# One layout for RWKV's block operands, its state part as 64-row products, and constant products ahead of others, in a hybrid encoder layer

## Chip, cores and metric

The kernel runs on one core of one Trainium2 chip. The metric is device microseconds (us) of one execution. Five engines work side by side, each in its own order: TensorE (PE in the profile; PEld is its weight loading), VectorE (DVE), ScalarE (ACT), GpSimd (POOL) and SyncE (SP), which issues most DMAs. TensorE's clock is granted at one of two levels, 1.2 or 2.4 GHz; "PEclk" in the profile is the mean granted clock of a stretch as a share of 2.4 GHz.

## What is computed

One encoder layer on 2048 tokens of width 1024, all in float32. Four mixers of 256 columns run on the projected input, their outputs are projected and added to x, and a mixture of 16 experts (each expert takes 256 tokens) follows.

```python
proj = jnp.einsum('btd,dc->btc', _rmsnorm(x, norm_mix[l]), w_in[l])
o_ret  = _retention_group(...)     # chunked retention, both directions
o_rwkv = _rwkv7_group(...)         # RWKV-7, both directions
o_lru  = _rglru_group(...)         # linear recurrence
o_gla  = _gla_group(...)           # gated linear attention, both directions
x = x + concat([o_ret, o_rwkv, o_lru, o_gla]) @ w_out[l]
x = x + _expert_choice_ffn(_rmsnorm(x, norm_ffn[l]), ...)
return _rmsnorm(x, norm_final)

# RWKV, one direction, per token and head (64 x 64 state S):
sa = jnp.einsum('bhvk,bhk->bhv', S, -kk_t)
S  = S * w_t[:, :, None, :] + sa[..., None] * (kk_t * a_t)[:, :, None, :] + v_t[..., None] * k_t[:, :, None, :]
y  = jnp.einsum('bhvk,bhk->bhv', S, r_t)
```

## The kernel before

The program is a series of stages: input projection, the linear recurrence, RWKV's first part (woven with more projection), then the stage that the change touches, then the output projection, the choice of tokens (`top_k`) and the experts.

The stage that the change touches weaves three generators with fixed weights: `rwkv_rest` (RWKV's second part, then the split of w_out and the first four tiles of the output projection), `retention` and `gla`. Each `yield` is a point at which the weave may go on with another generator. A scheduler then orders each engine's instructions from this list by its own estimate of readiness, so the order within an engine is fixed when the program is built; each engine executes its list in order and waits on semaphores.

RWKV's second part works on 16 blocks of 128 tokens (two chunks of 64) in two directions, so on 32 pairs (direction, block). `rwkv_load` fetches a pair's operands. `rwkv_prep` builds its matrix E in steps: p1 (four transposes, line 606), p2 (four transposes, line 615), R (four products on 64 rows of the array, line 628), the inner masks (four whole-array products, line 639), X (line 648) and E (four products of 256 columns, line 656). After each step ACT or DVE copies from the PSUM bank into the operand of a later step; before the change most of these copies work on 64 of the 128 partitions at a time, since the two chunks' halves lie crosswise (lines 610, 618, 633, 643). E = q1 - X q0, where q1 holds, beside computed parts, a constant identity and a DMA'd copy of r. `rwkv_chain` carries the state: per chunk four products E times mv (line 672), then a DVE product into the next mv (line 676) and an ACT copy of the output (line 680). RWKV has four PSUM banks of its own in rotation, retention and GLA two each.

A float32 product is executed in two passes and appears in the trace as two matmul records and two weight loads; a transpose as one.

Of the kernel before, what the change touches and what calls it, by code (L numbers as in the profile page):

```python
# [17 lines left out]
P = 128  # L18
# [4 lines left out]
NH = 4  # L23
# [513 lines left out]
def rwkv_b_buffers(g):  # L537

    nc = g.nc

    engines = [nc.vector, nc.gpsimd]

    def ring(name, shape, n, parts):
        ts = [g.fp.tile(shape, F32, name=f"{name}{i}") for i in range(n)]
        for i, t in enumerate(ts):
            for p in parts(t):
                engines[0].memset(p, 0.0)
                engines.reverse()
        return [ts, 0]

    def eye(t):
        for k, t1 in ((0, t[0:64, :, 0, 64:128]), (1, t[64:128, :, 1, 0:64])):
            nc.scalar.activation(out=t1, in_=g.c["eye64"][64 * k:64 * k + 64, None, :].broadcast_to([64, NH, C]), func=AF.Copy)
        return []
    g.rd = ring("rd", [P, 4, 2, C], 2, lambda t: [t[64 * k:64 * k + 64, :, 1 - k, :] for k in range(2)])
    g.q0 = ring("q0", [P, NH, 2, P], 2, lambda t: [t[64 * e:64 * e + 64, :, 1 - e, :] for e in range(2)])
    g.q1 = ring("q1", [P, NH, 2, P], 4, eye)
    g.ti = ring("ti", [P, NH, P], 4, lambda t: [t[64 * e:64 * e + 64, :, 64 - 64 * e:128 - 64 * e] for e in range(2)])
    g.mv = {}
# [7 lines left out]
def rwkv_load(g, dr, b):  # L567
# [14 lines left out]
    return ld, q1, ti  # L582


def rwkv_prep(g, dr, b, loaded, res):

    nc, c = g.nc, g.c
    ld, q1, ti = loaded  # L590
# [12 lines left out]
    for q in range(2):
        for e in range(2):
            o = (2 * q + e) * P
            nc.tensor.transpose(p1[:, o:o + P], bk[q][e], c["ident"])
    p1 = p1.rearrange("p (q e h c) -> p q e h c", q=2, e=2, h=2)
    for e in range(2):
# [3 lines left out]
    p2 = bank(g)  # L612
# [8 lines left out]
    rd = turn(g.rd)  # L621
    for k in range(2):
        nc.vector.tensor_copy(out=rd[H[k], :, k], in_=ld[H[k]].rearrange("p (u t) -> p u t", t=320)[:, :, 0:C])
    pss = [bank(g) for _ in range(2)]
    for q in range(2):
        for k in range(2):
            ks = ld[H[k], HALF * q:HALF * q + 384].rearrange("p (u t) -> p u t", t=C)[:, 1::3]
            nc.tensor.matmul(pss[k][:, q * P:(q + 1) * P], lhsT=z[q][H[k]], rhs=ks, start=True, stop=True)  # L628
    for k in range(2):
        pv = pss[k][:, 0:256].rearrange("p (q e t) -> p q e t", q=2, e=2)  # L630
        for e in range(2):
            s = H[e]
            nc.vector.tensor_tensor(out=R[s, k::2, H[1 - e]], in0=pv[s, :, 1 - e], in1=c["m_bm"][s, dr, None, :].broadcast_to([64, 2, C]), op=OP.mult)
    yield
    ps = bank(g)
    for q in range(2):
        for e in range(2):
            o = (2 * q + e) * P
            nc.tensor.matmul(ps[:, o:o + P], lhsT=bk[q][e], rhs=rd[:, 2 * q + 1 - e], start=True, stop=True)  # L639
    pv = ps.rearrange("p (q e h t) -> p q e h t", q=2, e=2, h=2)  # L640
    for e in range(2):
        for s, q in ((H[e], q0), (H[1 - e], q1)):
            nc.vector.tensor_tensor(out=qh(q[s, :, e, H[e]]), in0=pv[s, :, e], in1=c["m_in"][s, dr, None, None, :].broadcast_to([64, 2, 2, C]), op=OP.mult)
    yield

    ps = bank(g)
# [5 lines left out]
    E = g.ep.tile([P, NH, 2, P], F32, name="E", tag="E")  # L652
    for h2 in range(2):
        ps = bank(g)
        for h in range(2):
            nc.tensor.matmul(ps[:, h * 256:(h + 1) * 256], lhsT=X[:, 2 * h2 + h, :], rhs=q0[:, 2 * h2 + h].rearrange("p e c -> p (e c)"),  # L656
                             start=True, stop=True)
        s = slice(2 * h2, 2 * h2 + 2)
        nc.vector.tensor_tensor(out=E[:, s].rearrange("p h e c -> p (h e c)"), in0=q1[:, s].rearrange("p h e c -> p (h e c)"), in1=ps, op=OP.subtract)
        yield  # L660
# [1165 lines left out]
```

## Time and profile before

| | us |
|---|---|
| median of three runs | 2861.12 (2857.55 to 2868.86) |
| the profiled execution | 2858.58 |
| its span, first to last instruction | 2856.6 |
| RWKV's second part (lines 571 to 683) | from 836 to 1291 of the span |
| first and last matmul of the output projection | 1352.8 and 1626 |
| `top_k` begins, then the experts | 1633 |

Over the span PE is busy 91%, DVE 61%, ACT 49%, POOL 25%, and the mean granted clock is 0.947. Before 836 PE is busy 754 of 836 us and after 1633 it is busy 1162 of 1224 us, at 0.96 and 0.97 of the full clock. Between them the share of busy time and the clock are both lower. The section of rows below gives this stretch in six pieces. A busy share is to be read with the clock beside it, since a matmul at the lower clock is busy for longer. A piece of the PE timeline is a run of records of one line; the distance from its start to the start of the next piece, divided by its records, is what a record costs in the stream.

### The profile page before, as it was taken

To read this page: it belongs to the slowest core of one execution; us is meant where nothing else is said; L and a number is where in the kernel's file an instruction comes from. 1 tells how busy PE (TensorE), PEld (TensorE's weight loads), DVE (VectorE), ACT (ScalarE), POOL (GpSimd) and SP (SyncE) were. 2 spreads that over 40 slices of the span, in tenths; PEclk is the share of its full clock that TensorE was granted. 3 is DMA by queue.
4 is the path that set the end of the run, shared out by engine and by line. 5 is a ranking of instruction groups with operands and counts; after the bars stand their busy time and mean duration, and the time that the engine had idled before them with its cause. 6 is when DMAs were issued, how large, how long until landed. Compare 5 with 4: busy or idle time off the path is not lost.

```text
span 2856.6 us, 47428 instructions
## 1 busy us (share of the span) xinstructions
PE 2594.7 (91%) x18433; PEld 2321.6 (81%) x18433; DVE 1746.1 (61%) x3415; ACT 1392.3 (49%) x2348; POOL 711.5 (25%) x771
## 2 busy tenths in 40 slices
PE   6989998989888888886979859999999999999997
PEld 5866787768767777774767659999999999999987
DVE  4454567766887667788443475555555555566564
ACT  4366555435434676555533334444444444455453
POOL 0011115443524454347433200000000000000121
PEclk9999999999988889997989979999999999999999
DMA  8735554675446544446344346666666666789873
GB/s 304 278 101 190 182 164 151 203 231 166 136 122 177 161 153 148 145 127 190 107 143 171 127 147 206 205 206 205 206 205 205 205 206 206 228 289 298 266 238 140
DMA packets 474015, 538.40 MB, mean 188 GB/s; under 512 B 129952, under 2 KB 411584, under 8 KB 473024
## 3 DMA queue, kind: packets, MB, share of 16 engines
q1 hardware_dynamic: 461984, 492.12, 53.3%
q0 software_dynamic: 11808, 43.26, 5.8%
q8 instruction: 145, 2.38, 0.3%
q14 instruction: 78, 0.64, 0.1%
HBM read 392.17 MB, written 145.23 MB: 188 GB/s over the span
## 4 chain that ended last, share of the span: by engine, by line
PE 53%; DVE 5%; DMA 4%; ACT 3%; issue 2%; POOL 1%; SPq 0%; POOLq 0%; ACTq 0%; DVEq 0%
PE bank L129 43%; DMA rt_ld<-tm 1%; PE bank L656 1%; PE bank L1500 1%; PE bank L639 1%; DMA fn_x<-acc,x_idx 1%; PE bank L628 1%; PE bank L672 1%; PE bank L1481 1%; PE bank L648 1%; DVE tk_j L1395 0%; PE bank L1217 0%; PE bank L1323 0%; PE bank L960 0%; PE bank L952 0%
## 5 line engine op out<-in xcount | busy, mean ns | idle before, releaser
L44 DVE TENSOR_TENSOR x_wl<-x_st,x_wh 128x2048 fp32r<-128x2048 f32 x192 | 439.5, 2292 | 306.3 <-ACT x_wh L43 305.9
L129 PE MATMUL bank<-x_xh,x_wh 128*128 128x256 f32 x2048 | 580.2, 285 | 2.9 <-ACT x_wh L43 2.8
L129 PE MATMUL bank<-x_xl,x_wh 128*128 128x256 f32 x2048 | 577.4, 283 | 0.0
L129 PE MATMUL bank<-x_xh,x_wl 128*128 128x256 f32 x2048 | 572.2, 283 | 1.1 <-DVE x_wl L44 1.1
L43 ACT ACTIVATE x_wh<-x_st 128x2048 fp32r<-128x2048 f32 x192 | 367.0, 1913 | 106.7 <-PE bank L129 96.6
L129 PEld LDWEIGHTS bank<-x_xh,x_wh 128*128 128x128 f32 x2048 | 393.2, 192 | 3.6 <-ACT x_wh L43 3.2
L129 PEld LDWEIGHTS bank<-x_xl,x_wh 128*128 128x128 f32 x2048 | 393.3, 192 | 0.0
L129 PEld LDWEIGHTS bank<-x_xh,x_wl 128*128 128x128 f32 x2048 | 389.9, 192 | 1.5 <-DVE x_wl L44 1.5
L129 PE MATMUL bank<-x_wh,x_hh 128*128 128x256 f32 x1024 | 290.1, 285 | 4.8 <-ACT x_hh L43 4.8
L129 PE MATMUL bank<-x_wl,x_hh 128*128 128x256 f32 x1024 | 291.2, 285 | 0.0
L129 PE MATMUL bank<-x_wh,x_hl 128*128 128x256 f32 x1024 | 289.8, 284 | 0.0
L1626 POOL DMA_INDIRECT acc<-x_os,x_idx x30 | 48.9, 1631 | 926.8 <-ACT x_os L1560 899.0
L129 PE MATMUL bank<-h_hi,w_hi 128*128 128x512 f32 x576 | 238.5, 417 | 20.1 <-DVE o_cm L1676 13.8
L129 PE MATMUL bank<-h_lo,w_hi 128*128 128x512 f32 x576 | 240.0, 417 | 0.0
L129 PE MATMUL bank<-h_hi,w_lo 128*128 128x512 f32 x576 | 235.6, 409 | 0.0
L129 PEld LDWEIGHTS bank<-x_wh,x_hh 128*128 128x128 f32 x1024 | 196.6, 193 | 5.0 <-ACT x_hh L43 5.0
L129 PEld LDWEIGHTS bank<-x_wl,x_hh 128*128 128x128 f32 x1024 | 197.4, 193 | 0.0
L129 PEld LDWEIGHTS bank<-x_wh,x_hl 128*128 128x128 f32 x1024 | 197.2, 193 | 0.0
L129 PE MATMUL bank<-w_hi,h_hi 128*128 128x256 f32 (+1 forms) x512 | 156.4, 306 | 14.6 <-DVE o_tm L1676 11.8
L129 PEld LDWEIGHTS bank<-h_hi,w_hi 128*128 128x128 f32 x576 | 112.5, 196 | 56.3 <-DVE o_cm L1676 16.4
L129 PE MATMUL bank<-w_lo,h_hi 128*128 128x256 f32 (+1 forms) x512 | 149.4, 292 | 0.0
L129 PE MATMUL bank<-w_hi,h_lo 128*128 128x256 f32 (+1 forms) x512 | 148.8, 291 | 0.0
(457 smaller groups left out, 5490.2 us busy)
## 6 DMA issues: line engine op xcount, KB each, us to landing
x_st<-in_exp_w_gate_dram SPq DMA_DIRECT2D x64, 1024.0 KB, 8.4
x_st<-in_exp_w_up_dram SPq DMA_DIRECT2D x64, 1024.0 KB, 8.9
x_st<-in_exp_w_down_dram SPq DMA_DIRECT2D x64, 1024.0 KB, 5.5
w_st<-in_w_in_dram SPq DMA_DIRECT2D x20, 1024.0 KB, 6.7
rw_sp<-sp SPq DMA_DIRECT2D x16, 1280.0 KB, 4.6
bld<-rw_sp SPq DMA_DIRECT2D x32, 640.0 KB, 4.1
ld<-rw_cm SPq DMA_DIRECT2D x14, 899.5 KB, 6.1
cm<-o_cm SPq DMA_DIRECT2D x40, 256.0 KB, 2.8
```

The lines of the kernel that those rows point to most:

```text
L43: g.nc.scalar.activation(out=hi, in_=src, func=AF.Copy)
L44: (g.nc.gpsimd if pool else g.nc.vector).tensor_tensor(out=lo, in0=src, in1=hi.bitcast(F32), op=OP.subtract)
L129: g.nc.tensor.matmul(out, lhsT=lhs[a][:, k, lsl], rhs=rhs[b][:, k, rsl], start=(k + i == 0 and out is outs[0]), stop=(3 * k + i == 3 * nk ...
L628: nc.tensor.matmul(pss[k][:, q * P:(q + 1) * P], lhsT=z[q][H[k]], rhs=ks, start=True, stop=True)
L639: nc.tensor.matmul(ps[:, o:o + P], lhsT=bk[q][e], rhs=rd[:, 2 * q + 1 - e], start=True, stop=True)
L648: nc.tensor.matmul(ps[:, h * P:(h + 1) * P], lhsT=ti[:, h], rhs=R[:, h], start=True, stop=True)
L656: nc.tensor.matmul(ps[:, h * 256:(h + 1) * 256], lhsT=X[:, 2 * h2 + h, :], rhs=q0[:, 2 * h2 + h].rearrange("p e c -> p (e c)"), start=True ...
L672: nc.tensor.matmul(ps[:, h, :], lhsT=E[:, h, e, :], rhs=mv[e][:, h, :], start=True, stop=True)
L1481: nc.tensor.matmul(ps[:, 2 * s:2 * s + 2], lhsT=oh[:, i, s * P:(s + 1) * P], rhs=tok[:, i], start=(i == 0), stop=(i == NB - 1))
L1500: nc.tensor.transpose(ps[:, m * CAP + s * P:m * CAP + (s + 1) * P], xs[:, s, (k + m) * P:(k + m + 1) * P], c["ident"])
L1626: g.nc.gpsimd.indirect_dma_start(out=dst, out_offset=bass.IndirectOffsetOnAxis(ap=idx[:, s:s + 1], axis=0), in_=t[:, s], in_offset=None, **kw)
```

## The change

A helper `full` issues one bfloat16 product of 128 x 512 on a view of the identity into a bank, before the real products overwrite that bank. It stands ahead of six of the eight banks of `rwkv_prep` and of three per block of `retention` and of `gla`: 192 + 48 + 48 = 288 products.

In `rwkv_prep` the operands lie the same way on all 128 partitions: Q replaces q0 and q1, one copy replaces four (p1), one replaces two (R's left part), two products replace four (R's right part), one replaces four (masks). Per pair ACT issues 5 copies in place of 9, DVE 5 in place of 12. The two DVE copies into `rd` become two DMAs (64 in all) in `rwkv_load`. The R products become eight of 64 x 64, the E products sixteen of 64 x 64 with 128 columns. The constant identity and r leave E: `rwkv_chain` adds their part as products, per chunk one of `eye64` with 256 columns, four of `rq` with 64, and eight of E (128 rows, 64 columns of the array) where four whole-array products stood.

```diff
+def full(g, ps):
+    i = g.c["ident"].bitcast(BF16)
+    g.nc.tensor.matmul(ps.rearrange("p (a b) -> p a b", a=2), lhsT=i[:, 0:P], rhs=i[:, None, :].broadcast_to([P, 2, 2 * P]), start=True, stop=True)
+    return ps
 def rwkv_load(g, dr, b):
-            nc.sync.dma_start(out=q1[s, k::2, e, s], in_=half[64 * k:64 * k + 64, :, 320 - 320 * e:384 - 320 * e])
+    rd = turn(g.rd)
+    for k in range(2):
+        s = slice(64 * k, 64 * k + 64)
+        nc.sync.dma_start(out=rd[s, :, k], in_=sp[s].rearrange("p (u t) -> p u t", t=320)[:, :, 0:C])
 def rwkv_prep(g, dr, b, loaded, res):
-    for e in range(2):
-        for s, q in ((H[e], q0), (H[1 - e], q1)):
-            nc.scalar.activation(out=qh(q[s, :, e, H[1 - e]]), in_=p1[s, :, e], func=AF.Copy)
+            nc.sync.dma_start(out=rq[H[e], k::2], in_=half[H[k], :, 320 - 320 * e:384 - 320 * e])
+    p1 = full(g, bank(g))
...
+    nc.scalar.activation(out=Q[:, :, :, 0:C], in_=p1.rearrange("p (e h c) -> p e h c", e=2, h=NH), func=AF.Copy)
-        nc.scalar.activation(out=R[H[e], :, H[e]], in_=p2[H[e], 0], func=AF.Copy)
+    nc.scalar.activation(out=R[:, :, 0:C], in_=p2[:, 0], func=AF.Copy)
-        nc.vector.tensor_copy(out=rd[H[k], :, k], in_=ld[H[k]].rearrange("p (u t) -> p u t", t=320)[:, :, 0:C])
-    pss = [bank(g) for _ in range(2)]
+    pss = [full(g, bank(g)), bank(g)]
-            nc.tensor.matmul(pss[k][:, q * P:(q + 1) * P], lhsT=z[q][H[k]], rhs=ks, start=True, stop=True)
+                nc.tensor.matmul(pss[k][H[e], q * C:(q + 1) * C], lhsT=z[q][H[k], H[e]], rhs=ld[H[k], o:o + C], start=True, stop=True,
+                                 tile_position=(64 * k, 64 * e))
...
-            nc.tensor.matmul(ps[:, h * 256:(h + 1) * 256], lhsT=X[:, 2 * h2 + h, :], rhs=q0[:, 2 * h2 + h].rearrange("p e c -> p (e c)"),
-                             start=True, stop=True)
-        nc.vector.tensor_tensor(out=E[:, s].rearrange("p h e c -> p (h e c)"), in0=q1[:, s].rearrange("p h e c -> p (h e c)"), in1=ps, op=OP.subtract)
+    pss = [full(g, bank(g)), bank(g)]
+    for h in range(NH):
+        for u in range(2):
+            for e in range(2):
+                nc.tensor.matmul(pss[e][H[u], h * P:(h + 1) * P], lhsT=X[H[e], h, H[u ^ e]], rhs=Q[H[e], e, h], start=True, stop=True,
+                                 tile_position=(64 * e, 64 * u))
+        nc.vector.scalar_tensor_tensor(out=E[:, e].rearrange("p h c -> p (h c)"), in0=Q[:, e].rearrange("p h c -> p (h c)"), scalar=g.hm[:, e:e + 1],
+                                       in1=pss[e], op0=OP.mult, op1=OP.subtract)
 def rwkv_chain(g, dr, b, res):
-            nc.tensor.matmul(ps[:, h, :], lhsT=E[:, h, e, :], rhs=mv[e][:, h, :], start=True, stop=True)
+        nc.tensor.matmul(ps[H[1 - e]], lhsT=g.c["eye64"][H[e]], rhs=mv[e][H[e]], start=True, stop=False, tile_position=(64 * e, 64 - 64 * e))
+            nc.tensor.matmul(ps[H[e], h, :], lhsT=rq[H[e], h, :], rhs=mv[e][H[e], h, :], start=(h == 0), stop=False, tile_position=(64 * e, 64 * e))
+                nc.tensor.matmul(ps[c0:c0 + 64, h, :], lhsT=E[:, e, h, H[u]], rhs=mv[e][:, h, :], start=False, stop=(h == NH - 1), tile_position=(0, c0))
```

The changed file's lines are numbered 8 to 12 higher than before. Each engine's order changes with it. PE in the middle of RWKV's second part, before (X of two pairs, then E):

```order
L672 MATMUL bank<-mv_10039,E 128x64 x4
L648 MATMUL bank<-R,ti_7186 128x128 x4
L648 MATMUL bank<-R,ti_7187 128x128 x4
L656 MATMUL bank<-q_7166,X 128x256 x2
L656 MATMUL bank<-q_7167,X 128x256 x2
```

and after (L55 is `full`, L660 the E products, L1229 a score product of GLA, L964 one of retention):

```order
L1229 MATMUL bank<-gl_qx,gl_p 128x512
L660 MATMUL bank<-Q,X 64x128 x10
L55 LDWEIGHTS c_ident
L55 MATMUL bank<-c_ident 128x512
L660 MATMUL bank<-Q,X 64x128 x3
L964 MATMUL bank<-rt_qd_7360,rt_kT 128x256 x2
L55 LDWEIGHTS c_ident
L55 MATMUL bank<-c_ident 128x512
L660 MATMUL bank<-Q,X 64x128 x3
```

The constant products of other banks and whole-array products of the other generators now stand between the small ones. From the first pair to the last chain product the PE list goes from a whole-array product to one on part of the array, or back, 100 times before and 389 times after.

PE at the end of RWKV's second part, before (the last chain products, line 672, among retention, lines 938 to 960, and GLA, lines 1153 and 1159):

```order
L672 MATMUL bank<-mv_12550,E 128x64 x4
L672 MATMUL bank<-mv_12563,E 128x64 x4
L938 MATMUL bank<-c_ident,rt_a_10851 128x128 x4
L1153 MATMUL bank<-c_ident,gl_p 128x128 x2
L672 MATMUL bank<-mv_12551,E 128x64 x4
L672 MATMUL bank<-mv_12562,E 128x64 x4
L952 MATMUL bank<-rt_qd_7362,rt_kT 128x256 x2
L1159 MATMUL bank<-gl_v,gl_kt 32x64 x8
L960 MATMUL bank<-rt_sd_7366,rt_qs 128x128
```

and after (L790 and L792 are RWKV's output, L137 the output projection):

```order
L678 MATMUL bank<-mv_13590,c_eye_345 64x256
L680 MATMUL bank<-mv_13590,rq 64x64 x4
L684 MATMUL bank<-mv_13590,E 64x64 x8
L678 MATMUL bank<-mv_13605,c_eye_345 64x256
L680 MATMUL bank<-mv_13605,rq 64x64 x4
L684 MATMUL bank<-mv_13605,E 64x64 x8
L790 MATMUL bank<-c_ident,rw_y_13837 128x128 x4
L792 MATMUL bank<-xg,rw_g_up 128x256 x2
L137 MATMUL bank<-wo_hi,wo_mh 128x512
L137 MATMUL bank<-wo_lo,wo_mh 128x512
```

All score products of retention and GLA (32 each) now stand ahead of RWKV's last chain products; before, 20 and 16 of them did.

ACT in the middle of RWKV's second part, before (R's and mv's copies of two pairs, after a copy of GLA):

```order
L1111 ACTIVATE gl_xa<-bank 16x256
L618 ACTIVATE R<-bank 64x4x64
L619 ACTIVATE mv_10027<-bank 64x256
L618 ACTIVATE R<-bank 64x4x64
L619 ACTIVATE mv_10028<-bank 64x256
L618 ACTIVATE R<-bank 64x4x64
L619 ACTIVATE mv_10039<-bank 64x256
L618 ACTIVATE R<-bank 64x4x64
L619 ACTIVATE mv_10040<-bank 64x256
```

and after (L624 is R's copy, L626 mv's, L692 the chain's output):

```order
L692 ACTIVATE yt<-bank 64x256
L624 ACTIVATE R<-bank 128x4x64
L626 ACTIVATE mv_10512<-bank 64x256
L626 ACTIVATE mv_10513<-bank 64x256
L624 ACTIVATE R<-bank 128x4x64
L626 ACTIVATE mv_10528<-bank 64x256
L626 ACTIVATE mv_10529<-bank 64x256
```

One copy of R per pair stands where two stood.

## Rows read from the trace of the kernel before

**Rows 1.** Windows: engine busy (records), granted clock, DMA share, GB/s; six pieces.

```profile
core 0: us, PE busy (x) PEld busy (x) DVE busy (x) ACT busy (x) POOL busy (x), PEclk, DMA share, GB/s
836.00:866.00 30.00, 16.30 (x81) 13.45 (x80) 28.94 (x52) 10.39 (x27) 12.43 (x19) 0.70 0.52 155
866.00:1296.00 430.00, 375.67 (x2635) 322.88 (x2635) 321.62 (x802) 260.63 (x664) 196.93 (x297) 0.90 0.51 154
1296.00:1352.00 56.00, 31.30 (x127) 21.66 (x126) 50.32 (x87) 29.53 (x61) 44.45 (x35) 0.65 0.53 164
1352.00:1446.00 94.00, 88.30 (x518) 70.43 (x518) 43.17 (x122) 45.44 (x105) 43.54 (x44) 0.96 0.34 112
1446.00:1462.00 16.00, 0.85 (x14) 0.48 (x6) 9.36 (x22) 5.21 (x9) 7.21 (x4) 0.59 0.52 164
1462.00:1633.00 171.00, 165.74 (x906) 126.84 (x906) 65.70 (x234) 59.06 (x111) 56.67 (x73) 0.97 0.42 149
```

**Rows 2.** Waits, PE, 866 to 1296: who waited for whom, total us, times, longest.

```profile
PE bank L656 <- ACT X L650: 9.7, 5, 3.1
PE bank L628 <- DVE R L633: 6.9, 3, 3.5
PE bank L615 <- ACT q L610: 5.6, 6, 2.0
```

**Rows 3.** Groups by line, 836 to 1300: shapes, count | busy, mean ns | idle before.

```profile
L672 PE MATMUL bank<-mv,E 128*128 128x64 f32 x512 | 66.3, 279 | 4.2 <-DVE E L659 3.7 <-DVE mv L676 0.5
L656 PE MATMUL bank<-q,X 128*128 128x256 f32 x256 | 63.6, 399 | 12.5 <-ACT X L650 9.7 <-DVE q L643 2.7
L643 DVE TENSOR_TENSOR q<-bank,c_m_in 64x256 f32<-64x256 f32 x128 | 50.6, 419 | 7.2 <-PE bank L639 5.7
L610 ACT ACTIVATE q<-bank 64x256 f32<-64x256 f32 x128 | 43.8, 373 | 28.8 <-PE bank L606 27.7
L659 DVE TENSOR_TENSOR E<-q,bank 128x512 f32<-128x512 f32 x64 | 41.6, 680 | 4.7 <-PE bank L656 4.4
L633 DVE TENSOR_TENSOR R<-bank,c_m_bm 64x128 f32<-64x128 f32 x128 | 36.8, 288 | 15.3 <-PE bank L628 12.9 <-ACT R L618 0.3
L618 ACT ACTIVATE R<-bank 64x256 f32<-64x256 f32 x64 | 23.5, 368 | 2.2 <-PE bank L615 1.7 <-ACT xg L772 0.4
L623 DVE COPY rd<-bld 64x256 f32<-64x256 f32 x64 | 21.6, 338 | 9.4 <-DMA bld<-rw_sp 8.6
L650 ACT ACTIVATE X<-bank 128x512 f32<-128x512 f32 x32 | 18.5, 589 | 19.0 <-PE bank L648 18.7
```

**Rows 4.** PE timeline at 1002 to 1012, full clock: start, us, line, shape, records.

```profile
1002.27 0.43 PE L1159 MATMUL bank<-gl_v,gl_kt 128*32 128x64 f32 x16
1002.63 0.69 PE L1119 MATMUL bank<-gl_xa,gl_up 16*128 16x256 f32 x2
...
1005.84 2.86 PE L656 MATMUL bank<-q,X 128*128 128x256 f32 x12
1008.53 1.04 PE L606 MATMUL bank<-c_ident,bld 128*128 128x128 f32 x8
...
1009.85 1.90 PE L672 MATMUL bank<-mv,E 128*128 128x64 f32 x16
1011.59 0.61 PE L615 MATMUL bank<-c_ident,bld 128*128 128x128 f32 x4
```

**Rows 5.** PE timeline at 716, the stage before: 64-row products amid whole-array ones.

```profile
716.32 1.16 PE L448 MATMUL bank<-sp 64*128 64x128 f32 x16
717.41 0.39 PE L129 MATMUL bank<-w_lo,h_hi 128*128 128x256 f32 x1
717.64 0.28 PE L129 MATMUL bank<-w_hi,h_lo 128*128 128x256 f32 x1
717.76 0.28 PE L129 MATMUL bank<-w_hi,h_hi 128*128 128x256 f32 x1
```

**Rows 6.** PE timeline at 1622, output projection: 32-column products amid whole-array ones.

```profile
1621.69 0.39 PE L129 MATMUL bank<-wo_hi,wo_ml 128*128 128x512 f32 x1
1621.92 0.40 PE L129 MATMUL bank<-wo_hi,wo_mh 128*128 128x512 f32 x1
1622.25 0.43 PE L1328 MATMUL bank<-wo_hT,wo_rw 128*32 128x128 f32 x8
1622.61 0.50 PE L129 MATMUL bank<-wo_lo,wo_mh 128*128 128x512 f32 x1
1622.94 0.40 PE L129 MATMUL bank<-wo_hi,wo_ml 128*128 128x512 f32 x1
```

More of the change, by code (lines that the diff above doesn't have):

```diff
@@ L549, in ring @@
         return [ts, 0]
[L551 to L557, printed above, removed]
+    g.rd = ring("rd", [P, 4, 2, C], 4, lambda t: [t[64 * k:64 * k + 64, :, 1 - k, :] for k in range(2)])
     g.ti = ring("ti", [P, NH, P], 4, lambda t: [t[64 * e:64 * e + 64, :, 64 - 64 * e:128 - 64 * e] for e in range(2)])
+    g.hm = g.fp.tile([P, 2], F32, name="hm")
+    nc.vector.memset(g.hm, 1.0)
+    for e in range(2):
+        nc.vector.memset(g.hm[64 * e:64 * e + 64, e:e + 1], 0.0)
     g.mv = {}
@@ L625, in rwkv_prep @@
     for q in range(2):
         for k in range(2):
-            ks = ld[H[k], HALF * q:HALF * q + 384].rearrange("p (u t) -> p u t", t=C)[:, 1::3]
-            nc.tensor.matmul(pss[k][:, q * P:(q + 1) * P], lhsT=z[q][H[k]], rhs=ks, start=True, stop=True)
+            for e in range(2):
+                o = HALF * q + C + 3 * C * (1 - e)
+                nc.tensor.matmul(pss[k][H[e], q * C:(q + 1) * C], lhsT=z[q][H[k], H[e]], rhs=ld[H[k], o:o + C], start=True, stop=True,
+                                 tile_position=(64 * k, 64 * e))
@@ L629, in rwkv_prep @@
     for k in range(2):
[L630 to L633, printed above, removed]
+        nc.vector.tensor_tensor(out=R[:, k::2, C:P], in0=pss[k][:, 0:P].rearrange("p (q t) -> p q t", q=2),
+                                in1=c["m_bm"][:, dr, None, :].broadcast_to([P, 2, C]), op=OP.mult)
@@ L634, in rwkv_prep @@
     yield
[L635 to L638, printed above, removed]
+    ps = full(g, bank(g))
+    for e in range(2):
+        for q in range(2):
+            o = (2 * e + q) * P
             nc.tensor.matmul(ps[:, o:o + P], lhsT=bk[q][e], rhs=rd[:, 2 * q + 1 - e], start=True, stop=True)
[L640 to L643, printed above, removed]
+    nc.vector.tensor_tensor(out=Q.rearrange("p e h c -> p (e h) c")[:, :, C:P], in0=ps.rearrange("p (n t) -> p n t", t=C),
+                            in1=c["m_in"][:, dr, None, :].broadcast_to([P, 2 * NH, C]), op=OP.mult)
@@ L644, in rwkv_prep @@
     yield
-    ps = bank(g)
+    ps = full(g, bank(g))
     for h in range(NH):
@@ L935, in retention @@
             rot = rotate(g, pool, b, ld[:, 0:512], 2 * NH).rearrange("p h t -> p (h t)")
-            ps = bank(g)
+            ps = full(g, bank(g))
             for q in range(4):
@@ L949, in retention @@
             sd = [diag(S[0]), diag(SB[:, b])]
-            ps = bank(g)
+            ps = full(g, bank(g))
             for q in range(2):
@@ L955, in retention @@
             yield
-            ps = bank(g)
+            ps = full(g, bank(g))
             for q in range(2):
@@ L1215, in gla @@
                                         in1=c["gl_hq"][:, :, None].broadcast_to([P, NH, P]), op=OP.mult)
-                ps = bank(g)
+                ps = full(g, bank(g))
                 nc.tensor.matmul(ps, lhsT=o[:, 1, e, s], rhs=qx.rearrange("p h t -> p (h t)"), start=True, stop=True)
@@ L1230, in gla @@
             yield
-            ps = bank(g)
+            ps = full(g, bank(g))
             y = ps[:, 0:256]
```

45 lines of the change are left out of this document (20 added, 25 removed).

## The prediction

> **What bounds the kernel now.** I read the windows first, since a mean over 2857 us says nothing about one stage. They cut the stretch from 836 us (RWKV's second part begins) to 1633 us (the output projection ends) into six pieces [rows 1]. The reader is to see three things in them. PE's busy times add up to 678.2 us of 797, so 118.8 us are idle: 13.7, 54.3, 24.7, 5.7, 15.2 and 5.3 us by piece. No other engine comes near PE except in the third piece, where DVE is busy 50.3 and POOL 44.5 of 56 us. And the clock is down just where PE has gaps: 0.70, 0.90, 0.65 in the first three pieces, 0.96 and 0.97 where PE is busy nearly all the time. So the second piece, 430 us, is PE's: 375.7 us busy, DVE 321.6, ACT 260.6.
>
> A mean clock c means that 2(1-c) of the time ran at 1.2 GHz, and half of the busy time in it is excess. Busy time times (1-c) is therefore what the low clock costs: 4.9 + 37.6 + 11.0 + 3.5 = 57 us in the first four pieces.
>
> The waits say what PE's gaps are: a product waits for a copy that ACT or DVE has still to make, X for the E products, R for the next pair's R products, q for p2 [rows 2]. The groups give those copies, nearly all on 64 partitions [rows 3]. The timeline gives what a record costs in PE's stream at the full clock, which is less than its mean busy time, as neighbours overlap [rows 4].
>
> The time of the profiled execution is 2858.6 us, 2 us more than its span and 2.5 below the median of three. I make the sum against 2858.6. Outside 836 to 1633 no term changes: the projection before and the experts after have the same instructions.
>
> **The copies.** ACT, per pair: four copies of 373 ns become one of 128x512, 589 ns as X's, and two of 368 become one: 1.27 us less, 41 us over 32 pairs. DVE: two copies of 338 into rd go, four products of 419 become one of 680 as E's, four of 288 become two: 0.68 + 1.00 + 0.58 = 2.25 us less, 72 us in all [rows 3]. E's two subtractions keep their 128x512 shape. None of it is on the path by itself, for PE is the busier engine; its worth is shorter waits, counted under idle time. The 64 new DMAs into rd and those into rq (as many as went into q1) are issued by SP ahead of use; rd is loaded in the round before and first read three steps after p1, rq in the next round of blocks. With that cover and a DMA share of 0.51 [rows 1] I cost them at nothing; without it, the mask step would wait about as long as PE waits for copies today, 2 to 3 us a time [rows 2].
>
> **The small products.** Per pair the E products were 8 records of 2.69 / 12 = 0.224 us, 1.79 us [rows 4]. They become 32 records on 64x64 parts of the array with 128 columns. No row shows that shape. The nearest are products on 64 rows and 128 columns of the array, at two positions in turn: 16 records in 1.09 us, 68 ns each [rows 5]; and products on 32 columns at four positions, 16 in 0.36 us, 22 ns each [rows 4]. The new ones have four positions, like the second, and loads half as long as the first, so I take half of 68, 34 ns, and keep 22 and 68 as bounds. E: 1.09 us, 0.70 less. R: before, 8 records of 68 ns, after 16 of 34, no change. Chain, per pair 16 records in 1.74 us before [rows 4]. After, per chunk: the identity's two records of 256 columns as an E record before, 0.45 us; the eight records of rq on the other columns of the array beside them (the 22 ns show that column parts run side by side); 16 records of E at 34 ns, 0.54 us: 1.98 us per pair, 0.24 more. Sum: 32 x (-0.70 + 0.24) = -15 us. The 80 records per pair that count, 2560, make 2.6 us per ns: -31 us more at 22 ns, +87 at 68.
>
> **The constant products.** 288 records of 512 columns at the 0.23 us of a whole-array record of that width [rows 6]: +66 us of PE time. They need only a free bank, so they can run where PE would wait; I count them fully as work and take the cover off the idle time. If no gap covers them, the 66 us stand in full.
>
> **Going between parts and the whole array.** In the output projection a record starts 0.33 us after its neighbour instead of 0.23 both when the 32-column products begin and when they have ended [rows 6]; behind the 64-row products it is 0.23 instead of 0.12 [rows 5]. So a change costs 0.10 us. PE's list has 389 of them in place of 100: +29 us. At the least nothing, where PE waits anyway.
>
> **The clock.** Constant products use the whole array and fill gaps at the banks where PE waits today. Of the 57 us I take back 40. The bounds are 0 and 57; it is nearer to the upper one since the gaps that precede the low clock are the ones filled.
>
> **Idle time.** The start, 13.7 us, waits for the first DMA and stays 14. The second piece, 54 us, I put at 16: eleven copies fewer by ACT and DVE stand per pair before PE's products, and a constant product stands at most of the banks. The third piece's 25 us go to 15: w_out's split then has DVE and POOL nearly to itself, as retention and GLA are done by then in the new order, though PE has nothing of theirs left to do either. The 15 us at 1446 come after the last blocks of retention and GLA are written out and read back; those now come earlier, and 2 remain. The dense pieces keep 11. Together 58 in place of 119; bounds 45 and 95.
>
> **The sum.** Busy 678 - 15 + 66 + 29 - 40 = 718, idle 58: 776 in place of 797, so -21 us, and 2858.6 - 21 = **2838 us**, 0.7% less. A measurement of this kernel tells about 0.5%, 14 us, from no change, so the forecast lies not far beyond that.
>
> **Rivals.**
>
> *The small products don't run side by side (slower).* The place is the E products and the chain, the price is the ns per record. At 60 ns, near what 64-row products cost today [rows 5], the sum gains 26 x 2.6 = 67 us: 2838 + 67 = 2905. From 42 ns on the change is no gain, from 48 on slower by over 14 us. For it: the only row with 64 rows is at 68. Against it: that one loads 128 columns, and four 32-column positions do run side by side [rows 4].
>
> *The constant products don't raise the clock (the change does not do what it says).* If products that multiply mostly zeros, amid parts of the array, leave the granted clock at 0.90, the 40 us are not won: 2878. If PE's gaps then stay half filled too, another 20: about 2900. For it: the low clock stands beside waits for copies, which a product of 0.23 us does not bridge when they last 2 to 3 us [rows 2]. Against it: they are 288, at the banks with the waits.
>
> *No change.* The terms for and against are each 55 to 100 us and differ by 21. With 38 ns per record (+10) and 27 us of idle time left in the second piece (+11) they cancel: 2859.
>
> *Loads that stand in line (slower).* In the chain the E products use all rows of the array. If a weight load could not run under a matmul on the same rows, a record would cost its load, half of the 0.109 us of a whole-array record of 64 columns, and its matmul, a quarter of 0.224: 0.11 us. That is 16 x 0.076 = 1.2 us more per chunk, +78 over 64 chunks: 2916. Against it: by that mechanism the whole-array chain record of today would cost 0.109 + 0.056 = 0.165 us and it costs 0.109, and the 32-column products on all rows cost 22 ns [rows 4]. The Trainium skill has this rule ("TensorE: Matmul & The Clock Gate", Part 3, The mechanism): weight loads overlap matmuls in flight only when the row group differs. By that rule the time is the 2916 of this rival; the rows of this trace disagree with it.
>
> **How the numbers follow.** Chances: the forecast, 2785 to 2844, 0.46; no change, 0.20; small products dear, 0.19; clock not raised, 0.11; loads in line, 0.04. So faster 0.46, within 0.5% 0.20, slower 0.34. The two signs hold most of the chance between them; the likeliest case's own range is 2785 to 2844: its lower end has 22 ns per record (-31), all 57 us of the clock (-17) and half of the 0.10 us per change (-15), of which not all will come, and its upper end is the bound of a measurable gain. For 8 in 10 the range goes on through no change and most of the two slower rivals: 2785 to 2915.
>
> **What would show it.** Right: at the full clock E's 32 records take about 1.1 us from the first start to the next line's, a chunk's chain about 1.0; the mean clock between 866 us and RWKV's end is 0.95 or more and PE idle there is below 25 us; `full` is busy some 66 us; RWKV's last chain product comes near 1370 us, with retention and GLA done, and the output projection then needs about 240 us for its 16 tiles. Wrong: a price per record above 42 ns, a clock that stays at 0.90, or a second piece whose gaps only move to other banks. Shorter copies with unchanged waits would say that PE's order, not the copies, makes the gaps.

## The result, and the profile after

The changed kernel took 2898.53 us (median of four, 2896.74 to 2900.61) beside 2859.34 of the kernel before on the same chip. The ratio on record, which is not that of these two medians alone (1.0137), is 1.0122, with a 95% interval from 1.0104 to 1.0140. It is slower by 1.2%; the forecast was 2838, faster by 0.7%. The profiled execution took 2899.5 us, with a span of 2897.3.

The windows of the changed kernel, with the columns of [rows 1]; the pieces are the start, RWKV up to its last chain product, the hole behind it (PE waits, mostly for RWKV's output and the split of w_out), and the output projection up to `top_k`:

```profile
core 0: us, PE busy (x) PEld busy (x) DVE busy (x) ACT busy (x) POOL busy (x), PEclk, DMA share, GB/s
836.00:866.00 30.00, 18.47 (x199) 14.46 (x200) 29.53 (x44) 5.26 (x11) 8.75 (x11) 0.83 0.62 167
866.00:1413.00 547.00, 493.15 (x5319) 373.20 (x5315) 314.32 (x700) 283.25 (x670) 255.53 (x358) 0.95 0.50 145
1413.00:1426.00 13.00, 2.79 (x8) 1.92 (x8) 6.94 (x18) 4.60 (x4) 0.31 (x1) 0.50 0.89 270
1426.00:1669.40 243.40, 221.86 (x1202) 172.06 (x1202) 103.26 (x333) 77.87 (x152) 85.11 (x93) 0.96 0.43 144
```

The reader is to see three things. `top_k` now begins at 1669.4 instead of 1633.5: of the 41 us by which the span grew 36 are in this stretch, and 5 behind it, where no instruction changed. The clock did rise, from 0.90 to 0.95 in the long piece [rows 1]. And the long piece still has 53.9 us (547.00 - 493.15) in which PE is idle, as many as before (54.3).

I split each stretch, here and for every kernel below, into three parts: busy time times the clock (the work at the full clock), idle time, and busy time times (1 - clock). Before: 609 + 119 + 69 = 797 us. After: 698 + 97 + 38 = 833. Work rose by 89, idle time fell by 22, the low clock costs 31 less. Kernels with the same products differ by up to 24 us in the first of these parts (579, 591 and 603 below), so the work is good to some 10 us. The low clock is less firm: two traces of the changed kernel without its constants (executions of 2877.65 and 2896.08 us) differ by 5 us or less in work and idle time and by 10 to 15 in low clock. The sum of the parts is measured.

Groups by line of the changed kernel, 836 to 1413 (columns of [rows 3]). L55 is `full`, L660 E, L678 to L684 the chain, the rest the copies:

```profile
L55 PE MATMUL bank<-c_ident 128*128 128x512 bf16 x284 | 111.5, 399 | 18.9 <-DVE R L636 4.5 <-ACT mv L626 3.4 <-DVE E L663 3.2
L684 PE MATMUL bank<-mv,E 128*64 128x64 f32 x1024 | 53.2, 235 | 0.0
L660 PE MATMUL bank<-Q,X 64*64 64x128 f32 x1024 | 47.9, 286 | 3.9 <-ACT X L652 3.9
L680 PE MATMUL bank<-mv,rq 64*64 64x64 f32 x512 | 47.1, 229 | 0.0
L663 DVE SCALAR_TENSOR_TENSOR E<-Q,hm,bank 128x512 f32<-128x512 f32 x64 | 44.9, 741 | 4.5 <-PE bank L660 4.0
L678 PE MATMUL bank<-mv,c_eye 64*64 64x256 f32 x128 | 42.1, 410 | 7.8 <-DVE E L663 5.0 <-DVE mv L688 1.6 <-DVE hn_t L71 1.1
L644 DVE TENSOR_TENSOR Q<-bank,c_m_in 128x512 f32<-128x512 f32 x32 | 21.7, 685 | 14.7 <-PE bank L643 14.7
L617 ACT ACTIVATE Q<-bank 128x512 f32<-128x512 f32 x32 | 18.7, 595 | 46.3 <-PE bank L616 28.5 <-DVE E L663 17.5
L636 DVE TENSOR_TENSOR R<-bank,c_m_bm 128x128 f32<-128x128 f32 x64 | 17.0, 285 | 12.5 <-PE bank L633 12.0
```

The copies are what the change says: Q's at 595 and 685 ns stand for eight of 373 and 419 [rows 3]. The constants are busy 111.5 us by their own durations, which overlap, and 18.9 us of PE's idle time stand in front of the constants themselves: a constant must wait for its bank too, and what is behind it in PE's order waits with it. PE's longest waits, 866 to 1413 (columns of [rows 2]):

```profile
PE bank L921 <- POOL rt_kz L918: 6.3, 4, 2.5
PE bank L1248 <- POOL gl_sT L1241: 5.3, 4, 1.8
PE bank L678 <- DVE E L663: 5.0, 3, 2.9
PE bank L523 <- DVE E L663: 4.2, 1, 4.2
PE bank L995 <- DVE rt_y L89: 4.0, 3, 2.6
PE bank L660 <- ACT X L652: 3.9, 5, 1.6
```

The waits of [rows 2] did shrink: X's from 9.7 to 3.9, and those for R and q are not among the longest any more. Others took their place: retention's and GLA's products that wait for POOL, the chain that waits for E's copies, and the constants themselves.

The PE timeline of the changed kernel at the full clock (columns of [rows 4]):

```profile
890.31 0.69 PE L684 MATMUL bank<-mv,E 128*64 128x64 f32 x16
890.92 0.43 PE L678 MATMUL bank<-mv,c_eye 64*64 64x256 f32 x1
890.93 0.44 PE L680 MATMUL bank<-mv,rq 64*64 64x64 f32 x4
891.19 0.38 PE L678 MATMUL bank<-mv,c_eye 64*64 64x256 f32 x1
891.21 0.39 PE L680 MATMUL bank<-mv,rq 64*64 64x64 f32 x4
891.53 0.69 PE L684 MATMUL bank<-mv,E 128*64 128x64 f32 x16
892.15 0.39 PE L55 MATMUL bank<-c_ident 128*128 128x512 bf16 x1
...
1157.98 0.38 PE L55 MATMUL bank<-c_ident 128*128 128x512 bf16 x1
1158.19 0.49 PE L616 MATMUL bank<-c_ident,bld 128*128 128x128 f32 x3
1158.52 1.00 PE L1248 MATMUL bank<-gl_v,gl_sT 128*128 128x64 f32 x8
...
1159.58 0.27 PE L616 MATMUL bank<-c_ident,bld 128*128 128x128 f32 x1
1159.78 0.43 PE L678 MATMUL bank<-mv,c_eye 64*64 64x256 f32 x1
...
1282.56 1.10 PE L660 MATMUL bank<-Q,X 64*64 64x128 f32 x32
1283.60 0.39 PE L55 MATMUL bank<-c_ident 128*128 128x512 bf16 x1
```

A constant between two whole-array products takes 0.21 us (1157.98 to 1158.19). E's 32 records take 1.04 us, 32 ns each. The identity and rq of one chunk take 0.61 us (890.92 to 891.53), and the chunk's 16 records of E as long (to 892.15), 38 ns each. The three transposes at 1158.19 take 0.11 us each to the next start; the one at 1159.58, with the identity's product behind it, takes 0.20: the change to parts costs 0.09. In the single records the change back to a constant costs as much: E's last group of four records takes 0.22 us where the others take 0.11.

### The profile page after: what moved, and what is told of

Its sections match the earlier page's. It is cut to its first block, busy times and chain, and to the rows that moved or that the text cites. A ratio compares the mean times of both kernels' runs of the same rounds, so it can differ in the third digit from the quotient of the medians.

```text
span 2897.3 us, 51858 instructions
## 1 busy us (share of the span) xinstructions
PE 2655.1 (92%) x20897; PEld 2329.0 (80%) x20897; DVE 1684.2 (58%) x3194; ACT 1354.6 (47%) x2208; POOL 704.3 (24%) x771
## 4 chain that ended last, share of the span: by engine, by line
PE 55%; DVE 13%; DMA 11%; issue 5%; ACT 5%; POOL 3%; SPq 1%; POOLq 0%; DVEq 0%; ACTq 0%
PE bank L137 44%; DMA ld<-rw_cm 3%; DMA rt_ld<-tm 2%; PE bank L55 1%; DVE x L493 1%; PE bank L1512 1%; DMA fn_x<-acc,x_idx 1%; POOL pr L492 1%; PE bank L643 1%; DVE pr L492 1%; PE bank L684 1%; DMA mx<-go_g 1%; DMA go_g<-cm 1%; PE bank L1229 1%; PE bank L1493 1%
## 5 line engine op out<-in xcount | busy, mean ns | idle before, releaser
L137 PE MATMUL bank<-x_xh,x_wh 128*128 128x256 f32 x2048 | 581.6, 285 | 4.5 <-ACT x_wh L43 4.4
L137 PE MATMUL bank<-x_xl,x_wh 128*128 128x256 f32 x2048 | 578.9, 284 | 0.0
L137 PE MATMUL bank<-x_xh,x_wl 128*128 128x256 f32 x2048 | 573.3, 284 | 0.4 <-DVE x_wl L44 0.4
L137 PEld LDWEIGHTS bank<-x_xh,x_wh 128*128 128x128 f32 x2048 | 394.8, 193 | 5.3 <-ACT x_wh L43 4.8
L137 PEld LDWEIGHTS bank<-x_xl,x_wh 128*128 128x128 f32 x2048 | 394.7, 193 | 0.0
L137 PEld LDWEIGHTS bank<-x_xh,x_wl 128*128 128x128 f32 x2048 | 391.3, 193 | 0.6 <-DVE x_wl L44 0.6
L137 PE MATMUL bank<-x_wh,x_hh 128*128 128x256 f32 x1024 | 290.1, 285 | 5.0 <-ACT x_hh L43 5.0
L137 PE MATMUL bank<-x_wl,x_hh 128*128 128x256 f32 x1024 | 291.3, 285 | 0.0
L137 PE MATMUL bank<-x_wh,x_hl 128*128 128x256 f32 x1024 | 289.8, 284 | 0.0
L137 PE MATMUL bank<-h_hi,w_hi 128*128 128x512 f32 x576 | 237.1, 414 | 18.6 <-DVE o_cm L1688 11.8
L137 PE MATMUL bank<-h_lo,w_hi 128*128 128x512 f32 x576 | 239.4, 416 | 0.0
L137 PE MATMUL bank<-h_hi,w_lo 128*128 128x512 f32 x576 | 234.0, 407 | 0.0
L137 PEld LDWEIGHTS bank<-x_wh,x_hh 128*128 128x128 f32 x1024 | 196.6, 193 | 5.2 <-ACT x_hh L43 5.2
L137 PEld LDWEIGHTS bank<-x_wl,x_hh 128*128 128x128 f32 x1024 | 197.5, 193 | 0.0
L137 PEld LDWEIGHTS bank<-x_wh,x_hl 128*128 128x128 f32 x1024 | 197.4, 193 | 0.0
L137 PE MATMUL bank<-w_hi,h_hi 128*128 128x256 f32 (+1 forms) x512 | 156.5, 306 | 11.0 <-DVE o_tm L1688 8.5
L137 PEld LDWEIGHTS bank<-h_hi,w_hi 128*128 128x128 f32 x576 | 111.8, 194 | 55.0 <-DVE o_cm L1688 14.5
L137 PE MATMUL bank<-w_lo,h_hi 128*128 128x256 f32 (+1 forms) x512 | 149.2, 291 | 0.0
L137 PE MATMUL bank<-w_hi,h_lo 128*128 128x256 f32 (+1 forms) x512 | 148.8, 291 | 0.0
```

The lines of the kernel that those rows point to most:

```text
L137: g.nc.tensor.matmul(out, lhsT=lhs[a][:, k, lsl], rhs=rhs[b][:, k, rsl], start=(k + i == 0 and out is outs[0]), stop=(3 * k + i == 3 * nk ...
```

## Experiments: the constants

All kernels beside the kernel before, with the three parts of the stretch from 836 us to `top_k` in their traces (sum: its length). "Fold" is explained below. The parts of e1 are those of e15's trace, the same kernel at its usual time. Differences in us below are differences of these ratios times 2860.

| kernel | median us | ratio, 95% interval | work | idle | low clock |
|---|---|---|---|---|---|
| before | 2859 to 2866 | 1 | 609 | 119 | 69 |
| changed | 2898.5 | 1.0122 (1.0104-1.0140) | 698 | 97 | 38 |
| e1 no constants | 2880.0 | 1.0048 (1.0031-1.0064) | 629 | 115 | 71 |
| e2 before + 288 constants | 2885.6 | 1.0066 (1.0050-1.0083) | 687 | 94 | 46 |
| e3 fold | 2884.2 | 1.0051 (1.0033-1.0069) | 652 | 110 | 57 |
| e4 fold, no constants | 2850.2 | 0.9953 (0.9936-0.9969) | 582 | 146 | 56 |
| e5 = e4 + old copies' work | 2864.3 | 0.9998 (0.9984-1.0013) | 592 | 139 | 73 |
| e6 constants of 128 columns | 2888.5 | 1.0080 (1.0059-1.0100) | 660 | 110 | 55 |
| e7 = e4, chunks a step later | 2846.4 | 0.9934 (0.9912-0.9956) | 579 | 135 | 68 |
| e8 = e4, whole-array chain | 2859.4 | 0.9979 (0.9966-0.9992) | 596 | 127 | 71 |
| e9 before + small E | 2867.3 | 1.0017 (1.0001-1.0034) | 608 | 134 | 57 |
| e10 = e7, fold on GpSimd | 2880.2 | 1.0055 (1.0041-1.0069) | 589 | 139 | 92 |
| e11 96 constants | 2897.0 | 1.0107 (1.0079-1.0136) | 657 | 117 | 65 |
| e12 192 constants | 2894.0 | 1.0104 (1.0077-1.0131) | 681 | 101 | 47 |
| e13 = e7 + 192 constants | 2874.4 | 1.0038 (1.0020-1.0056) | 629 | 124 | 57 |
| e14 = e7, E by halves | 2842.1 | 0.9924 (0.9900-0.9949) | 591 | 126 | 57 |
| e15 = e1 again | 2878.7 | 1.0059 (1.0040-1.0078) | 629 | 115 | 71 |
| e16 = e9, E by halves | 2868.0 | 1.0022 (1.0007-1.0037) | 620 | 116 | 68 |
| e17 = e14, R by halves | 2846.6 | 0.9945 (0.9928-0.9962) | 603 | 126 | 49 |

**Without any, and alone.** e1 and e15 leave the product out of `full`; e2 puts `full` at the same banks of the kernel before.

```diff
-    g.nc.tensor.matmul(ps.rearrange("p (a b) -> p a b", a=2), lhsT=i[:, 0:P], rhs=i[:, None, :].broadcast_to([P, 2, 2 * P]), start=True, stop=True)
     return ps
```

> The changed kernel without its 288 constant products; all else stays. Theory 1 (the constants are paid: 288 x 0.23 = 66 us of TensorE time that stands in line with the real products, against some 25 us that the higher clock gives back): about 2858 us, 40 below the changed kernel, with the mean clock of RWKV's stretch back at 0.90 to 0.92. Theory 2 (the constants come out even, the small products with their changes between parts and the whole array are what costs): 2890 to 2905. Theory 3 (the constants are what holds the changed kernel up): 2910 or more, with the clock at 0.88 or lower.

> The kernel before with the 288 constant products alone, at the same banks (six per direction and block of RWKV, three per block of retention and of GLA). Theory 1: 2859 + 66 - 25 = about 2900 us, the clock near 0.95. Theory 2: 2850 to 2865. Theory 3: 2830 or less.

> The changed kernel without its 288 constants, once more, for a trace at its usual time: 2880 us; against the trace of the changed kernel some 70 us less work at the full clock, and about 50 us more in waits and low clock together.

Taken away, they give 21 us back (1.0122 to 1.0048, by 2860 us; 18 by e15); put alone into the kernel before, they cost 19. So they cost about 20 us in these two kernels (in the folded one, below, 28: e3 against e4), and of the loss of 35 half or somewhat more is theirs. The size lies between theories 1 and 2. The windows of the second trace without them:

```profile
836.00:866.00 30.00, 16.89 (x164) 14.86 (x162) 29.39 (x46) 5.16 (x11) 7.84 (x17) 0.72 0.61 166
866.00:1375.00 509.00, 449.62 (x5008) 359.84 (x5010) 300.36 (x674) 271.16 (x652) 237.47 (x347) 0.87 0.52 147
1375.00:1424.00 49.00, 17.28 (x87) 13.21 (x83) 40.03 (x67) 19.37 (x25) 33.55 (x21) 0.65 0.69 217
1424.00:1651.00 227.00, 216.58 (x1203) 168.99 (x1201) 92.16 (x315) 73.71 (x148) 72.57 (x87) 0.99 0.42 144
```

To be seen: a clock of 0.87 against 0.95, and 115 us idle in all against 97. The 288 constants are 69 us of work (0.24 each); the clock gives 33 back, idle time 18. Of these 18 only 5.5 are in the long piece (59.4 to 53.9); 10.4 are behind it, where RWKV ends 38 us later. How the gain divides between clock and idle time is not firm: in e2 it is 23 and 25 for 78 of work, in the folded kernel (e3 against e4) none and 36 for 70. The work is much the same in all three, and more than what comes back. Theory 3 falls.

**Smaller ones.** e6 has `ps[:, 0:P]` and `rhs=i[:, 0:P]`, 128 columns.

> The changed kernel with constants of 128 columns in place of 512. Theory 1 (a constant costs its columns): the work falls from some 70 us to about 20; if the clock keeps what it gained the time is 2850 to 2865, if the clock falls back as it does without them it is about 2885. If a constant costs by being there (a change of the array's parts, a place in line) and not by its columns: 2895.

2888.5: 9 us above none, 12 below the full size. The work is 31 us (0.11 each), the clock gives 16 back and idle time 5. A quarter of the columns has nearly half the cost and, by the parts, nearly half the effect; neither size pays.

**Part of them.** e11 keeps those of retention and GLA, e12 those of RWKV, e13 puts the latter into the fastest kernel at that time.

> The changed kernel without the 192 constants of RWKV; the 96 of retention and GLA stay. If every constant costs alike (288 cost 19 us against none): about 2886. If those of retention and GLA, which stand where TensorE waits for GpSimd, are the ones that fill gaps: 2875 to 2882. If they are the dear ones: 2892 or more.

> The changed kernel without the 96 constants of retention and GLA; the 192 of RWKV stay (the other half of the run with 96). If RWKV's constants are covered by its waits and the clock they give back: 2876 to 2884, as without any. If they gain by themselves: below 2876. If the two sorts don't add up (whichever come first cost, the others are then covered): 2890 to 2900.

> The fastest kernel so far (fold, chunks a step later, no constants: 2846 us) with RWKV's 192 constants. If these are covered by waits there too: 2840 to 2850. If constants cost as all 288 did in the folded kernel (+34): about 2868.

e11 alone had the look of an answer: 96 constants cost 17 us, nearly as much as all (21), so RWKV's 192 would be free. e12 refutes it: these cost 16 alone, and 30 in the folded kernel (e13). By these figures the costs don't add up: whichever sort stands alone costs 16 or 17, the second sort on top 4 or 5. But the intervals of e11 and e12 are 8 us to either side, and the gap of 12 us between 17 + 16 and 21 is no more than these and the other two intervals leave open, so this is not shown. In the parts the clock cost falls 71, 65, 47, 38 for 0, 96, 192, 288 constants and the work rises 629, 657, 681, 698.

## Experiments: the state's part and the copies

**The fold** (e3 with, e4 without constants). The changed kernel adds the identity and rq in the chain, by products; the kernel before held them in E. The fold subtracts E from a tile `wq` that holds both:

```diff
-        nc.vector.scalar_tensor_tensor(out=E[:, e]..., in0=Q[:, e]..., scalar=g.hm[:, e:e + 1], in1=pss[e], op0=OP.mult, op1=OP.subtract)
+        for s, t in ((H[e], wq), (H[1 - e], Q[:, e])):
+            nc.vector.tensor_tensor(out=E[s, e]..., in0=t[s]..., in1=pss[e][s], op=OP.subtract)
...
-        nc.tensor.matmul(ps[H[1 - e]], lhsT=g.c["eye64"][H[e]], rhs=mv[e][H[e]], ...)
-        for h in range(NH):
-            nc.tensor.matmul(ps[H[e], h, :], lhsT=rq[H[e], h, :], rhs=mv[e][H[e], h, :], ...)
```

> The changed kernel with its constants, but the identity and rq are folded into E again: E is subtracted from a tile that holds them, in four VectorE operations on 64 partitions in place of two on 128, and the chain keeps only its E products. It takes the identity's and rq's products (about 0.61 us per chunk of both directions, 64 chunks, 39 us of TensorE time) and adds 2 x 0.68 us of VectorE time per direction and block, 44 us beside other work. Theory 2: about 2860 us, 39 below the changed kernel. Theory 1: TensorE's time counts there too, 2860 to 2875. If the chain's products only take the place of waits: 2890 to 2900.

> The same fold, without the constants. Theory 1: 2899 - 40 - 39 = about 2820 us, faster than the kernel before. Theory 2: like the fold with the constants, about 2860. If less work only makes more waits and a lower clock: 2850 or more.

The fold gains 20 us with constants and 27 without. It takes 46 and 47 us of work from PE, and a part of that comes back as idle time (97 to 110, 115 to 146), with constants also as low clock (38 to 57). e4 is the first kernel that beats the one before. TensorE's time for the identity and rq alone, 64 x 0.61 = 39 us, would have gained more than the 27.

**The copies.** e5 gives e4 the old copies' work back, unread: three `activation(out=g.j1[0:64], in_=p1[0:64, 0:256])`, three `tensor_copy` from the R products and three from the mask products per pair.

> The kernel with the fold and without constants (2850 us), to which the work of the old copies is given back as copies that nobody reads: three more ACT copies from p1 on 64 partitions x 256 per direction and block (about 1.1 us), three VectorE copies from the R products (0.3 us each) and three from the mask products (0.4 us each), about 2.1 us, together 100 us of ACT and VectorE time. If the one-layout copies are what the changed kernel gains by (shorter waits of TensorE for them): 2862 or more. If the copies are beside the path, as the unchanged idle time of the changed kernel suggests: 2845 to 2856.

The long piece of e4 and that of e5:

```profile
866.00:1307.00 441.00, 357.60 (x4199) 284.69 (x4197) 304.62 (x666) 246.44 (x593) 214.81 (x321) 0.90 0.56 161
866.00:1366.00 500.00, 413.88 (x4424) 330.42 (x4424) 382.46 (x920) 297.88 (x744) 243.00 (x347) 0.86 0.52 149
```

By the sums of all windows 58 us of DVE and 26 of ACT came to 13 us of time: 0.16 us per us. The one-layout copies do gain, but little, and not by PE's idle time: with the old copies' work back the long piece has 86 us of it, without 83, and the whole stretch 139 and 146. The parts show the rest as low clock (73 against 56) and work (592 against 582), differences no larger than what these parts can tell.

**The chain's form and place.** e8 computes it on the whole array (`ps[:, h, :]`, `lhsT=E[:, e, h, :]`, E's columns in the order of the outputs); e7 puts one `yield` ahead of each chain.

> The kernel with the fold and without constants, with the chain's products on the whole array again: per chunk of both directions 16 records of 0.109 us in place of 32 of 0.038 (1.74 and 1.22 us; 64 half chunks, so about 32 x 0.52 = 17 us more work), and 77 changes fewer (8 us less). By these prices: 2855 to 2862. If changes cost more than 0.10 us: 2850 or less. If the small products are what the changed kernel gains by: 2870 or more.

> The kernel with the fold and without constants, each chunk of the chain one step later, beside the products of R and of E, which also use parts of the array. TensorE's list then changes between parts and the whole array about 24 times less (222 in place of 246). By the price of 0.10 us that is 2 us: 2845 to 2852. If the order of the steps sets the waits: outside 2838 to 2860.

The small chain is worth 7 us (intervals that overlap a little), near the 9 of the prices (17 less 8). e7's 5 us are within the intervals.

**E alone.** e9 is the kernel before with E's products as in L660; e16 and e14 do all of the first column half before the second; e17 the same for R.

```diff
...
-        for h in range(2):
-            nc.tensor.matmul(ps[:, h * 256:(h + 1) * 256], lhsT=X[:, 2 * h2 + h, :], rhs=q0[:, 2 * h2 + h]..., start=True, stop=True)
+    for h in range(NH):
+        for u in range(2):
+            for e in range(2):
+                nc.tensor.matmul(pss[e][H[u], h * P:(h + 1) * P], lhsT=X[H[e], h, H[u]], rhs=q0[H[e], h, e], ..., tile_position=(64 * e, 64 * u))
```

> The kernel before with the E products alone in the new form: 32 records on 64x64 parts in place of 8 on the whole array, two banks by column half, the two subtractions in their old shape; copies and chain as before, no constants. By the prices read in the changed kernel (1.02 us against 1.79 per direction and block, 70 changes more at 0.10 us) TensorE does 25 - 7 = 18 us less: about 2846. If what a stage of RWKV waits for is its copies and banks and not TensorE: 2856 to 2866.

> The kernel before with small E products alone (2867 us with the halves mixed), here the first column half's 16 records first, then the second's. If the holding of E's two banks ate the 18 us that E's products save: 2846 to 2856. If the order of the halves is worth what it was in the folded kernel (4 us): 2860 to 2866. If waits on copies take whatever PE saves: 2864 to 2870.

> The fastest kernel so far (2846 us) with E's products in another order: all of the first column half, then all of the second, so that the first bank can go to VectorE while TensorE fills the second. If the holding of E's two banks is what eats the saving: 2836 to 2842. If the products lose by it what they had by running on all four parts (32 ns a record, at most twice that: 32 x 1.02 = 33 us): 2850 to 2880. If neither: 2843 to 2849.

> The fastest kernel so far (2842 us), with R's products by half too and E's halves in the order in which the chain of each direction asks for them. If R's two banks are held as E's were: 2836 to 2840. If not: 2840 to 2845. If R's products lose by running on two parts in place of four: 2846 or more.

The group of E in e9, 836 to 1322, and behind it the longest of PE's waits there, 866 to 1300, and the same wait in the kernel before, 866 to 1296:

```profile
L657 PE MATMUL bank<-q,X 64*64 64x128 f32 x1024 | 47.2, 288 | 9.2 <-ACT X L650 7.1 <-DVE q L643 2.1
```

```profile
PE bank L606 <- DVE E L660: 10.4, 7, 4.4
PE bank L606 <- DVE E L659: 1.1, 2, 0.7
```

E's group fell from 63.6 us [rows 3] to 47.2, and the kernel is not faster (1.0017). p1 (L606) now waits 10.4 us for E's copies, where it waited 1.1: E holds two banks until DVE has read both. But the order by halves, which lets the first bank go earlier, changes nothing (e16: 1.0022, and the same wait is 12.0); in the folded kernel it and R's are within the intervals (e14, e17). So it is not the order of the halves that makes the wait; that DVE makes it is argued, not tested. Where E's saving goes is shown only in part, and some 60 to 70 more changes between parts and the whole array (160 in the trace of e9, 102 in that of the kernel before; 70 in the expectation of e9), about 6 us at 0.09, are all else that I can name.

**Another engine for the fold.** e10 leaves E's two DVE operations whole and lets GpSimd add `wq`.

> The kernel with the fold, the later chunks and no constants (2846 us), but E is subtracted in two VectorE operations on 128 partitions, as in the changed kernel, and GpSimd adds the identity and rq to its half afterwards: 44 us less on VectorE, some 60 us more on GpSimd, which is off the path for a round; E's two banks come free after two copies instead of four. If banks that wait for VectorE's E copies hold TensorE up (11 us of its waits in the folded kernel): 2835 to 2842. If not: 2844 to 2850. If the wait for GpSimd lands in the chain: 2855 or more.

Slower by 35 us than e7. Its waits, 866 to 1318:

```profile
PE bank L687 <- POOL E L669: 11.4, 9, 4.3
PE bank L620 <- DVE E L667: 8.3, 4, 4.6
```

The chain waits for GpSimd, which has retention's and GLA's work in its line, but most of the loss stands under another part: idle time is 4 us more than in e7, work 10, and the low clock costs 92 us in place of 68. A round of distance was no cover.

**The kernel with the lowest time** is e14 (small products, one-layout copies, fold, chunks a step later, E by halves, no constants): 2842 us, 0.9924 of the kernel before; the intervals of e4, e7 and e17 overlap with its own. Its windows:

```profile
836.00:866.00 30.00, 16.14 (x156) 14.23 (x154) 29.42 (x41) 6.37 (x15) 10.94 (x18) 0.71 0.67 177
866.00:1295.00 429.00, 362.65 (x4161) 296.69 (x4162) 304.77 (x658) 244.25 (x578) 208.43 (x315) 0.89 0.58 163
1295.00:1363.00 68.00, 33.78 (x163) 25.51 (x162) 55.57 (x114) 31.49 (x65) 35.91 (x32) 0.70 0.63 196
1363.00:1609.70 246.70, 235.29 (x1328) 182.97 (x1326) 105.96 (x346) 95.09 (x189) 98.37 (x108) 0.99 0.41 140
```

It has about the clock of the kernel before (0.89) and more idle time (126 us), and is faster by its 18 us less work and its 12 us less of low clock, against 7 more idle.

## Why the prediction was wrong

**Idle time: the step that failed.** It put 119 us down to 58; 97 stayed. Of the 39 us that are missing nearly all are in the second piece, which was to fall from 54 to 16 and stayed at 53.9; the later pieces came as foretold (31.7 us behind RWKV, 28 forecast). Both reasons for the 16 fell short. With "eleven copies fewer" and no constants the second piece has 59.4 us of idle time, 5 more than before, and e5, which gives such copies' work back, leaves the idle time where it was. "A constant product stands at most of the banks" took 5.5 us in this piece, for a constant waits for its bank like the product behind it (18.9 us in front of L55). The prediction named this sign: "a second piece whose gaps only move to other banks". Its last sentence would put them down to PE's order; that is not shown, for the orders tried (e7, e14, e16, e17) changed little.

**The clock: right in kind, 9 us short.** It rose to 0.95 in the long piece as foretold. 31 of the 40 us came, and by these traces the constants brought them: without them the low clock costs 71, with them 38. So the second rival, a clock that is not raised, is wrong in its mechanism. That its 2900 is near the time is luck, though its second half, gaps that stay, is what came.

**The constants: right.** 66 us of work forecast, 69 measured. The cover that the prediction counted under idle time is what was missing: 18 us of idle time went with the constants.

**The small products: right in price, the chain mis-sized.** E's records cost 32 ns, forecast 34, below the 42 of the first rival. The chain's chunk was to cost 0.99 us and costs 0.61 for the identity and rq and 0.61 for E (16 records of 38 ns): rq's records do run beside the identity's, but these two cost 0.61, not 0.45. That is 64 x 0.23 = 15 us. The single records say why: rq's last record takes 0.15 us to the start of E's first, where the others take 0.06; E's records start in pairs 0.06 us apart, and the last pair before another shape takes 0.16. To go from one part shape to another thus costs the same 0.09 as to go to or from the whole array, and the 389 changes of the prediction are of the second kind alone; of the first kind the trace has 139, the one before 18, and 121 x 0.09 = 11 us. Where E's products stand alone in the chain (e13), 32 of them take 1.08 us and not 2 x 0.61:

```profile
1318.38 1.15 PE L683 MATMUL bank<-mv,E 128*64 128x64 f32 x32
1319.46 0.39 PE L55 MATMUL bank<-c_ident 128*128 128x512 bf16 x1
```

That the whole term was -15 hid a choice: it holds 64 x 0.45 = 29 us for the identity and rq, and without them (39 us by their measured 0.61) e4 is 27 us faster. With the changes the sum was +14; the trace without constants has +20.

**Loads in line: wrong as said.** The chain's E records use all rows and cost 38 ns, not 0.11 us. By the rule of the Trainium skill ("TensorE: Matmul & The Clock Gate", Part 3, The mechanism: loads overlap matmuls in flight only when the row group differs) the chain would have taken 1.2 us more per chunk; the trace disagrees.

**The sum.** 9 us too low for the work, 9 for the clock, 39 for idle time, and 5 behind the stretch: 62, against 2899.5 - 2838 = 61.5. In time the runs divide the loss so: the constants 21 us (1.0122 to 1.0048), the state's part as products 27 (1.0048 to 0.9953), and what is left of the change, copies and small products, is a gain of 13. Taken in the other order the state's part is 20 and the constants 28.

## To carry to other kernels

Products that only raise TensorE's clock cost their whole time on the engine that bounds the stage: here 69 us of work for some 50 of clock and idle time; a run without them tells at once. A stage whose gaps are single waits in a line of dependent steps need not lose its gaps when copies get shorter: here a sixth of the copies' time came through. What an engine with time to spare can fold into an operand (VectorE here; with GpSimd in its place the kernel was 35 us slower) should not become products on the one without.

## What was not expected of the hardware

Constants of 128 columns cost 0.11 us of work each, twice their columns' share of the 0.24 that 512 cost. The timeline of e6 at the full clock shows where the rest can lie:

```profile
987.46 0.23 PE L55 MATMUL bank<-c_ident 128*128 128x128 bf16 x1
987.62 0.72 PE L633 MATMUL bank<-bld 64*64 64x64 f32 x16
...
994.64 0.22 PE L55 MATMUL bank<-c_ident 128*128 128x128 bf16 x1
994.70 1.11 PE L650 MATMUL bank<-R,ti 128*128 128x128 f32 x8
```

Between whole-array products such a constant takes 0.06 us, its columns' share of 0.21; ahead of products on parts it takes 0.16. In the traces PE goes between parts and the whole array 295 times without constants (e15) and 398 times with these. So of the 31 us of work 288 x 0.06 = 17 are the constants, and 103 x 0.09 = 9 the changes that they bring. The second surprise is that a change between two part shapes, inside the chain, costs as much as one to the whole array.
